# Recurrence steps of a two-layer hybrid block: products of even and odd heads placed in the two column halves of the array, with the state read directly

## The chip, the core and the metric

The kernel runs on one core of a Trainium2 chip. The metric is device time in microseconds (us) of one execution; lower is better. Three runs of the kernel before gave 2442.71, 2450.8 and 2458.3 us, a median of 2450.8 us.

## The reference

Two transformer layers run over 512 latent tokens and 256 context tokens of width 1024. Each layer has a mixing part (a WKV-7 recurrence with 8 heads of 64 in two directions, beside differential attention with 8 heads), an output projection, and a squared-ReLU MLP. All arithmetic is float32. The part that matters here is the recurrence, for each head and each direction:

```python
def step(state, inp):
    r_t, w_t, k_t, v_t, kk_t, b_t = inp
    sa = jnp.einsum("bhvk,bhk->bhv", state, kk_t)
    state = (state * w_t[:, :, None, :]
             - sa[..., :, None] * b_t[:, :, None, :]
             + v_t[..., :, None] * k_t[:, :, None, :])
    y = jnp.einsum("bhvk,bhk->bhv", state, r_t)
    return state, y
```

The context is scanned first and its last state starts the scan of the latent tokens. The second direction scans in reverse, and the two results are added. In the last layer the context's outputs are not needed.

## The kernel before, in words

**Chunks.** The recurrence does not go token by token. The 768 tokens are six blocks of 128 (`n` = 0 to 5), each two chunks of 64 (`j` = 0, 1). One call `step(n, j)` advances both directions (`d` = 0, 1) by one chunk, so a layer has 12 steps and 24 step-directions, and the program has 48. With the decays folded into the operands, a chunk is a few 64-wide matrix products and one triangular inverse per head.

**What is prepared.** `prep_a` and `prep_b` make a set of four tiles for each (n, d): `KR` (columns 0 to 63 hold the scaled kk, 64 to 127 the scaled r), `BN`, the decay column `dcv`, and `G`. `G` has, for each chunk and head, rows 64 to 127 for products with v, rows 0 to 63 for products with the solved u, columns 0 to 63 for the solve and 64 to 127 for y. There are six sets in turn, so block n + 3 writes where block n was. The upper left quarter of `G` must become the inverse of a unit triangular matrix: `relay` sends its diagonal blocks to DRAM, `inv` loads them with one system per partition, `eliminate` solves them by 30 pairs of vector operations (on POOL for n < 2, on DVE after), the result goes back through DRAM into rows 0 to 63 of `G` (L1137), and `merge` fills the off-diagonal block with 64 small matmuls and two copies (L1152 to L1165).

**One step.** For each direction:

- L1176 loads v into partitions 64 to 127 of `uv`, on SP's queue.
- L1186 multiplies rows 64 to 127 of `G` (64 rows of the array) by v for 8 heads, all into partitions 0 to 63 of the PSUM tile `X` (128 x 512), one head after the other along the free axis. The first of the 8 has 128 output columns, since it also clears the lower half.
- L1189 adds the state's part for two heads at a time: `KR` with 128 output columns (kk and r together) against `sbd`, a block diagonal copy of the state with 128 columns per pair of heads.
- L1192 copies the upper half of `X`, negated, into `xs` (one ACT operation of 64 x 512).
- L1198 applies the inverse to `xs`; even heads go to partitions 0 to 63 of a PSUM tile `us`, odd heads to 64 to 127. Two ACT copies (L1201) put the result into partitions 0 to 63 of `uv`.
- L1210 makes the state's increment, again with even and odd heads in the two halves; L1213 and L1215 (DVE) form the new state `sc`, and two ACT copies (L1218) refresh `sbd`.
- L1226 adds the products with u and v for y into partitions 64 to 127 of `X`; L1236 (ACT) or L1239 (DVE) takes y out.

**Order.** Each engine runs its instructions in a fixed order that a list scheduler made from the program's order and its own estimate of times. In the program, the steps are generators; at each of their pauses the code lets four pieces of `preps` go (for block n + 2) and, at the first pause of a step, four pieces of the modulation weights (`ada`, 0.5 MB each, matmuls at L265, loads at L254 on SP's queue, kept behind the load of v). `inv(n + 1)` stands ahead of block n's steps. `finish` normalizes y for a finished block and starts with the last additions to y; its transposes are L1288.

Of the kernel before, what the change touches and what calls it, by code (L numbers as in the profile page):

```python
# [164 lines left out]
class K:  # L165
# [760 lines left out]
    def recurrence(self, l, last, es, side):  # L926
# [7 lines left out]
        one = self.pool(es, "one", 1)  # L934
# [232 lines left out]
        def step(n, j):  # L1167
            need_y = not (last and n < 2)
            final = n == 5 and j == 1
            mw = 128 if need_y else 64  # L1170
            S = []
            for d in range(2):
                q = j if d == 0 else 1 - j
                t0 = tau(n, d) * 128 + q * 64
                uv = uvp.tile([128, 8, 64], F32, name=self.n("uv"), tag=f"uv{d}", bufs=2)
                ld = nc.sync.dma_start(uv[64:128], self.vnd[t0:t0 + 64, :].rearrange("t (h c) -> t h c", h=8))  # L1176
                self.gate = ld
                KR, BN, G, dcv = sets[(n, d)]
                S.append(dict(q=q, t0=t0, uv=uv, KR=KR, BN=BN, G=G, dc=dcv))
            for d in range(2):  # L1180
                s = S[d]
                q = s["q"]
                X = s["X"] = px[d].tile([128, 512], F32, name=self.n("X"), tag=f"X{d}")
                for h in range(8):
                    w = mw if h == 0 else 64
                    nc.tensor.matmul(X[0:w, h * 64:h * 64 + 64], s["G"][64:128, h - h % 2 + q, h % 2, 0:w],  # L1186
                                     s["uv"][64:128, h, :], start=(h == 0), stop=False, skip_group_check=True)
                for p in range(4):
                    nc.tensor.matmul(X[0:mw, p * 128:p * 128 + 128], s["KR"][:, 2 * p + q, 0:mw], sbd[:, d, p, :],  # L1189
                                     start=False, stop=False, skip_group_check=True)  # L1190
                xs = s["xs"] = xsd[d]
                nc.scalar.mul(xs[0:64], X[0:64, :], -1.0)  # L1192
                yield
            for d in range(2):
                s = S[d]
                up = us[:, d]
                for h in range(8):
                    nc.tensor.matmul(up[(h % 2) * 64:(h % 2) * 64 + 64, h // 2, :], s["G"][:, h - h % 2 + s["q"], h % 2, 0:64],  # L1198
                                     s["xs"][:, h * 64:h * 64 + 64], start=True, stop=True, skip_group_check=True)
                for hf in range(2):  # L1200
                    nc.scalar.copy(s["uv"][0:64, hf:8:2, :], up[hf * 64:hf * 64 + 64])  # L1201
                yield
            if not final:
                for d in range(2):
                    s = S[d]
                    q = s["q"]
                    sp = us[:, d]
                    for h in range(8):
                        hs = slice((h % 2) * 64, (h % 2) * 64 + 64)
                        nc.tensor.matmul(sp[hs, h // 2, :], s["BN"][:, h - h % 2 + q, hs], s["uv"][:, h, :],  # L1210
                                         start=True, stop=True, skip_group_check=True)
                    tt = uvp.tile([128, 4, 64], F32, name=self.n("st"), tag="st")
                    nc.vector.tensor_tensor(tt, sp, sc[d], ALU.add)  # L1213
                    dcv = s["dc"][:, q:8:2].unsqueeze(2).to_broadcast([128, 4, 64])
                    nc.vector.tensor_tensor(sc[d], tt, dcv, ALU.mult)  # L1215
                    for hf in range(2):
                        hs = slice(hf * 64, hf * 64 + 64)
                        nc.scalar.copy(sbd[hs, d, :, hs], sc[d][hs])  # L1218
                    yield
            if need_y:  # L1220
                for d in range(2):
                    s = S[d]
                    X = s["X"]
                    for h in range(8):
                        ks = slice(0, 64 if h == 0 else 128)
# [7 lines left out]
                    yo = Yt[hp * 64:hp * 64 + 64, :]  # L1233
                    if hp not in seen:
                        seen[hp] = 1
                        nc.scalar.copy(yo, X[64:128, :])  # L1236
                    else:
                        seen[hp] = 2
                        nc.vector.tensor_tensor(yo, X[64:128, :], yo, ALU.add)  # L1239
                    if len(seen) == 2 and min(seen.values()) == 2:  # L1240
                        done.append(ti)
                    yield

        def finish(ti):
# [57 lines left out]
            yield from inv(1)  # L1302

        def rest():
            nonlocal uvp, fp, px, us, xsd
# [3 lines left out]
            xsd = [uvp.tile([128, 512], F32, name=self.n("xs"), bufs=1) for _ in range(2)]  # L1309
# [5 lines left out]
            us = self.pool(es, "pus", 1, PSUM).tile([128, 2, 4, 64], F32, name=self.n("us"))  # L1315
            pms.append(self.pool(es, "pmr", 1, PSUM))
            ada = Fill()
            kinds = (("mix", "rows"), ("mlp", "cols"), ("mlp", "rows"))
            for kd, how in kinds:
                ada.add((self.ada_rows if how == "rows" else self.ada_cols)(l, kd, pa, "a"))  # L1320
            if l == 0:
                ada.add(self.ada_cols(1, "mix", pa, "a"))
            work = Fill()
            prep_until(1)
            for n in range(6):
                if n == 0:
                    merge(0)
                    merge(1)
                elif n < 5:
                    self.now(inv(n + 1))  # L1330
                for j in range(2):
                    nst = 0
                    for _ in step(n, j):
                        work(1)
                        if nst == 0:
                            with tc.issue_after(self.gate.ins):
                                ada(ADA[l])
                        nst += 1

# [12 lines left out]

        done, spare = [], []
        uvp = fp = px = us = xsd = None
        side.add(prologue())
        return rest

# [379 lines left out]
```

## Time and profile before

| | before |
|---|---|
| median of three runs | 2450.8 us |
| the profiled execution | 2465.64 us, span 2463.9 us |
| TensorE matmul busy, whole span | 92% |
| VectorE / ScalarE / GpSimd busy | 62% / 48% / 33% |
| 16 DMA engines | 127 GB/s mean |

The profile tells of one execution. Times in rows are from the start of its span. The steps of the first layer's recurrence run from about 490 to 763 us and those of the second layer's from about 1760 to 2047 us; windows with these bounds are used below. A float32 matmul appears as two records, so a group of 8 heads is "x16". Matmuls are pipelined: the start of one record to the start of the next tells how long it holds the array, while its shown duration includes its way through the array. PEclk is the granted TensorE clock as a share of 2.4 GHz; it takes one of two levels, 1.2 or 2.4 GHz, so a mean of 0.77 is a mixture of both.

### The profile page before, as it was taken

How to read it: one execution, taken by the hardware profiler on the slowest of the kernel's cores; microseconds unless marked ns; L12 is line 12 of the kernel's file. 1: busy time of each engine (PE TensorE's matmuls, PEld its weight loads, DVE VectorE, ACT ScalarE, POOL GpSimd, SP SyncE). 2: the span in 40 equal slices, each digit the busy share in tenths (PEclk: the TensorE clock that was granted, in tenths of full speed). 3: DMA queues.
4: the chain of work that ended last, by engine and by line, in shares of the span. 5: the costliest groups of instructions: out<-in, count | busy, mean ns of one | idle time of the engine just before them, and what ended most of it. 6: DMA issues, size and time to landing. Idle time of an engine off the chain costs nothing.

```text
span 2463.9 us, 43744 instructions
## 1 busy us (share of the span) xinstructions
PE 2273.2 (92%) x17150; PEld 1919.2 (78%) x17150; DVE 1516.6 (62%) x2629; ACT 1173.8 (48%) x2393; POOL 806.8 (33%) x1048
## 2 busy tenths in 40 slices
PE   6999998799989999999999989999989978999997
PEld 5887887677768988888888877788767758888886
DVE  5456458558654665555555646657556564778784
ACT  4345547554534543344343535547444444555452
POOL 1212324832111333333330422423641131553530
PEclk8999998798899999999999999999678879999998
DMA  7543535386687422221112354434566663423230
GB/s 270 154 129 94 133 110 140 74 228 172 148 208 236 152 77 69 69 69 61 60 61 85 124 164 122 122 108 115 148 158 158 166 161 137 161 91 117 87 119 35
DMA packets 291630, 313.67 MB, mean 127 GB/s; under 512 B 139680, under 2 KB 220896, under 8 KB 291424
## 3 DMA queue, kind: packets, MB, share of 16 engines
q1 hardware_dynamic: 280320, 284.66, 38.6%
q0 software_dynamic: 10240, 23.08, 5.0%
q8 instruction: 135, 2.21, 0.4%
q10 hardware_dynamic: 864, 3.15, 0.3%
q14 instruction: 71, 0.58, 0.1%
HBM read 257.04 MB, written 53.77 MB: 126 GB/s over the span
## 4 chain that ended last, share of the span: by engine, by line
PE 68%; DMA 10%; DVE 9%; ACT 4%; issue 3%; SPq 2%; POOL 2%; POOLq 0%; DVEq 0%; ACTq 0%
PE pf L351 31%; PE pu L351 15%; PE po L351 4%; DMA raw<-in_ada_w 2%; PE pb L1046 2%; PE po L832 2%; DMA TT<-dt 2%; PE X L1186 1%; PE pb L977 1%; PE adar L265 1%; PE sc L795 1%; DVE wl L1497 1%; PE X L1226 1%; DVE nm L797 1%; PE X L1189 1%
## 5 line engine op out<-in xcount | busy, mean ns | idle before, releaser
L1497 DVE TENSOR_TENSOR wl<-raw,wh 128x1024 fp32r<-128x1024 f32 x170 | 255.8, 1507 | 125.6 <-ACT wh L1496 124.8
L351 PE MATMUL pf<-hl,wh 128*128 128x512 f32 (+1 forms) x832 | 282.1, 342 | 0.0
L351 PE MATMUL pf<-hh,wh 128*128 128x512 f32 (+1 forms) x832 | 280.5, 342 | 0.5 <-ACT hh L397 0.5
L351 PE MATMUL pf<-hh,wl 128*128 128x512 f32 (+1 forms) x832 | 275.7, 342 | 0.0
L1496 ACT ACTIVATE wh<-raw 128x1024 fp32r<-128x1024 f32 x170 | 179.2, 1058 | 162.0 <-PE pf L351 143.9
L351 PE MATMUL pf<-wh,fah 128*128 128x512 f32 x570 | 225.3, 398 | 11.5 <-DVE fu L1630 7.2
L351 PE MATMUL pu<-hh,wh 128*128 128x512 f32 (+1 forms) x632 | 223.5, 354 | 4.8 <-DVE t L557 1.7
L351 PE MATMUL pf<-wl,fah 128*128 128x512 f32 x570 | 225.0, 396 | 0.7 <-DVE wl L1497 0.7
L351 PE MATMUL pf<-wh,fal 128*128 128x512 f32 x570 | 222.8, 397 | 1.8 <-DVE fal L1597 1.8
L351 PE MATMUL pu<-hh,wl 128*128 128x512 f32 (+1 forms) x632 | 218.1, 346 | 4.4 <-DVE wl L340 4.4
L351 PE MATMUL pu<-hl,wh 128*128 128x512 f32 (+1 forms) x632 | 217.8, 345 | 0.0
L797 DVE TENSOR_REDUCE nm<-sc 128x1 f32<-128x768 f32 (+1 forms) x160 | 132.6, 842 | 79.2 <-PE sc L795 78.5
L351 PEld LDWEIGHTS pf<-hl,wh 128*128 128x128 f32 x832 | 156.6, 188 | 20.0 <-DVE hl L399 0.2
L351 PEld LDWEIGHTS pf<-hh,wl 128*128 128x128 f32 x832 | 156.0, 188 | 20.0
L351 PEld LDWEIGHTS pf<-hh,wh 128*128 128x128 f32 x832 | 155.3, 188 | 20.4 <-ACT hh L397 0.8
L799 ACT ACTIVATE e<-sc,nm 128x768 f32<-128x768 f32 (+1 forms) x160 | 130.7, 821 | 53.7 <-DVE nm L797 44.3
L321 POOL TENSOR_TENSOR rs<-ms,pw 128x1 f32<-128x1 f32 (+2 forms) x60 | 56.8, 948 | 286.3 <-DVE ms L319 284.5
L351 PEld LDWEIGHTS pu<-hh,wh 128*128 128x128 f32 x632 | 121.0, 191 | 23.8 <-DVE t L557 2.3
L351 PEld LDWEIGHTS pf<-wh,fah 128*128 128x128 f32 x570 | 107.7, 189 | 38.9 <-ACT fah L1596 13.7
L1630 DVE TENSOR_TENSOR acc<-pf,acc 128x512 f32<-128x512 f32 x155 | 104.2, 682 | 53.9 <-PE pf L351 53.3
L351 PEld LDWEIGHTS pu<-hh,wl 128*128 128x128 f32 x632 | 120.7, 191 | 19.5 <-DVE wl L340 5.3
L351 PEld LDWEIGHTS pu<-hl,wh 128*128 128x128 f32 x632 | 120.8, 191 | 14.2 <-issue 1.7
(262 smaller groups left out, 5644.1 us busy)
## 6 DMA issues: line engine op xcount, KB each, us to landing
raw<-in_w_ff SPq DMA_DIRECT2D x128, 512.0 KB, 3.7
raw<-in_ada_w SPq DMA_DIRECT2D x96, 512.0 KB, 5.8
raw<-in_w_in SPq DMA_DIRECT2D x52, 512.0 KB, 4.6
ld<-zd SPq DMA_DIRECT2D x40, 384.0 KB, 3.9
ks<-qd POOLq DMA_DIRECT2D x64, 192.0 KB, 5.8
zd<-zr SPq DMA_DIRECT2D x22, 384.0 KB
raw<-in_w_out SPq DMA_DIRECT2D x16, 512.0 KB, 5.9
qs<-qd POOLq DMA_DIRECT2D x32, 192.0 KB, 6.0
```

Of the source, the lines that this page charges most:

```text
L265: nc.tensor.matmul(acc[32 * g:32 * g + 32, :], self.sc[:, 2 * kp + k, :], raw[:, k, g * 128:g * 128 + 128], start=(kp + k == 0), stop=(kp ...
L321: nc.gpsimd.tensor_tensor(r, m, self.pw1.to_broadcast([128, cols]), ALU.pow)
L351: nc.tensor.matmul(out, a, b, start=(start and i == 0 and j == 0), stop=(i == n - 1 and j == 2), skip_group_check=not start)
L795: nc.tensor.matmul(sc[:, k0:k1], qs[:, br, tk], ks[:, br, k0:k1], start=True, stop=True)
L797: nc.vector.tensor_reduce(nm, sc, AX.X, ALU.max, negate=True)
L799: nc.scalar.activation(ee, sc, AF.Exp, bias=nm, accum_out=ls[:, br:br + 1])
L832: nc.tensor.matmul(po, pT[:, k * 128:k * 128 + 128], vn[:, k, h * 64:h * 64 + 64], start=(k == 0), stop=(k == nk - 1))
L977: nc.tensor.matmul(pw[:, p, :, :], wab[:, d, cs], lt, start=True, stop=True, skip_group_check=True)
L1046: nc.tensor.matmul(pgt[:, u, 0:nn], BK[hs, u, :], KR[hs, 2 * pp + u, 0:nn], start=True, stop=True, skip_group_check=True)
L1496: nc.scalar.activation(hi, src, AF.Copy)
L1497: nc.vector.tensor_tensor(lo, src, hi.bitcast(F32), sub)
L1630: nc.vector.tensor_tensor(d, p, d, add)
```

## The change

The products of L1186 and of y are placed like those of L1198: even heads into partitions 0 to 63 and odd heads into 64 to 127, with all 128 rows of `G`; the u half of `uv` is first set to zero by POOL. The state's part is now eight products of 64 x 64 straight from `sc` (`from_state`), once for the solve and once for y; `sbd` and its copies go. The state has two buffers. Each direction has a PSUM bank that holds X and then u and the increment; y has a bank of its own, one for both directions. Y's layout in SBUF follows, and the transposes in `finish` become 16 products of 64 x 64.

```diff
-        sbd = one.tile([128, 2, 4, 128], F32, name=self.n("sbd"))
-        nc.gpsimd.memset(sbd, 0.0)
-        sc = [one.tile([128, 4, 64], F32, name=self.n("sc")) for _ in range(2)]
+        state = lambda d: one.tile([128, 4, 64], F32, name=self.n("sc"), tag=f"sc{d}", bufs=2)
+        sc = [state(d) for d in range(2)]
...
+                nc.gpsimd.memset(uv[0:64], 0.0)
...
+            def from_state(out, s, c0):
+                for h in range(8):
+                    hs = half(h)
+                    nc.tensor.matmul(out[hs, h // 2, :], s["KR"][hs, h - h % 2 + s["q"], c0:c0 + 64], s["old"][hs, h // 2, :],
+                                     start=False, stop=False, skip_group_check=True)
...
-                X = s["X"] = px[d].tile([128, 512], F32, name=self.n("X"), tag=f"X{d}")
+                X = s["X"] = px[d].tile([128, 2, 4, 64], F32, name=self.n("X"), tag=f"X{d}")
                 for h in range(8):
-                    w = mw if h == 0 else 64
-                    nc.tensor.matmul(X[0:w, h * 64:h * 64 + 64], s["G"][64:128, h - h % 2 + q, h % 2, 0:w],
-                                     s["uv"][64:128, h, :], start=(h == 0), stop=False, skip_group_check=True)
-                for p in range(4):
-                    nc.tensor.matmul(X[0:mw, p * 128:p * 128 + 128], s["KR"][:, 2 * p + q, 0:mw], sbd[:, d, p, :],
-                                     start=False, stop=False, skip_group_check=True)
+                    nc.tensor.matmul(X[half(h), 0, h // 2, :], s["G"][:, h - h % 2 + s["q"], h % 2, 0:64],
+                                     s["uv"][:, h, :], start=(h < 2), stop=False, skip_group_check=True)
+                from_state(X[:, 0], s, 0)
                 xs = s["xs"] = xsd[d]
-                nc.scalar.mul(xs[0:64], X[0:64, :], -1.0)
+                for hf in range(2):
+                    nc.scalar.mul(xs[0:64, hf], X[hf * 64:hf * 64 + 64, 0], -1.0)
...
-                up = us[:, d]
+                up = s["X"][:, 1]
...
+                    sc[d] = state(d)
                     nc.vector.tensor_tensor(sc[d], tt, dcv, ALU.mult)
-                    for hf in range(2):
-                        hs = slice(hf * 64, hf * 64 + 64)
-                        nc.scalar.copy(sbd[hs, d, :, hs], sc[d][hs])
...
-                    X = s["X"]
+                    Y = yp.tile([128, 4, 64], F32, name=self.n("Yb"), tag="Yb")
                     for h in range(8):
-                        ks = slice(0, 64 if h == 0 else 128)
-                        nc.tensor.matmul(X[64:128, h * 64:h * 64 + 64],
-                                         s["G"][ks, h - h % 2 + s["q"], h % 2, 64:128],
-                                         s["uv"][ks, h, :], start=False, stop=(h == 7), skip_group_check=True)
+                        nc.tensor.matmul(Y[half(h), h // 2, :], s["G"][:, h - h % 2 + s["q"], h % 2, 64:128],
+                                         s["uv"][:, h, :], start=(h < 2), stop=False, skip_group_check=True)
+                    from_state(Y, s, 64)
...
-                        nc.scalar.copy(yo, X[64:128, :])
+                        nc.scalar.copy(yo, Y)
...
-                nc.tensor.transpose(pt[:, p, :], Yt[:, p * 128:p * 128 + 128], self.ident)
+                for hp in range(2):
+                    for hf in range(2):
+                        hs = slice(hf * 64, hf * 64 + 64)
+                        c0 = hp * 256 + p * 64
+                        nc.tensor.matmul(pt[hs, p, hp * 64:hp * 64 + 64], Yt[hs, c0:c0 + 64], self.ident[hs, hs],
+                                         start=True, stop=True, skip_group_check=True)
```

## Rows read from the trace of the kernel before

**Rows 1.** Busy us (count) of PE, PEld, DVE, ACT, POOL; PEclk, DMA share, GB/s.

```profile
490.00:763.00 273.00, 244.22 (x3496) 195.72 (x3495) 170.63 (x463) 130.65 (x310) 69.59 (x122) 0.90 0.77 198
1760.00:2047.00 287.00, 248.31 (x3250) 203.85 (x3249) 158.96 (x435) 121.76 (x286) 80.39 (x170) 0.77 0.60 151
```

**Rows 2.** Chain of waits by line, 490 to 763, then 1760 to 2047.

```profile
by line: DMA raw<-in_ada_w 10.0%; PE pb L1046 7.3%; DMA TT<-dt 7.2%; PE X L1226 6.1%; PE adar L265 5.7%; PE X L1186 4.0%; PE pb L977 3.5%; DMA raw<-in_w_out 3.4%; DMA S<-gd 3.2%; DMA da<-S 3.0%; issue 3.0%; PE X L1189 2.9%; PE us L1198 2.9%
...
by line: PE X L1186 9.0%; PE adar L265 6.0%; PE pb L1046 5.8%; PE X L1189 5.7%; issue 5.1%; PE pb L977 5.0%; DMA TT<-dt 4.9%; DMA raw<-in_ada_w 4.6%; PE X L1226 4.3%; DMA S<-zd 4.1%; PE us L1198 3.7%; PE us L1210 2.9%; DVE pr L1100 2.9%; DM
```

**Rows 3.** Both stretches summed, for L1186, L1189, L1226 in this order.

```profile
sum 560.00, PE 77.20 PEld 64.68; mean PE 38.60 PEld 32.34
...
sum 560.00, PE 63.08 PEld 53.06; mean PE 31.54 PEld 26.53
...
sum 560.00, PE 56.06 PEld 47.00; mean PE 28.03 PEld 23.50
```

**Rows 4.** Timeline of PE, full clock: start, us, line, tiles, rows*columns, records.

```profile
704.97 0.69 PE L1210 MATMUL us<-uv,S 128*64 128x64 f32 x16
705.58 0.42 PE L265 MATMUL adar<-raw,sc 128*32 128x128 f32 x6
705.93 1.39 PE L1186 MATMUL X<-uv,S 64*128 64x64 f32 x16
707.25 2.05 PE L1189 MATMUL X<-sbd,S 128*128 128x128 f32 x16
...
713.98 0.32 PE L1226 MATMUL X<-uv,S 64*64 64x64 f32 x2
714.24 0.69 PE L1210 MATMUL us<-uv,S 128*64 128x64 f32 x16
714.76 0.98 PE L1226 MATMUL X<-uv,S 128*64 128x64 f32 x14
715.67 1.39 PE L1186 MATMUL X<-uv,S 64*128 64x64 f32 x16
```

**Rows 5.** Timeline of PE inside a merge, record by record.

```profile
691.33 0.19 PE L1154 MATMUL pg<-TT,S 32*32 32x32 f32 x1
691.34 0.19 PE L1152 MATMUL pg<-TT,S 32*32 32x32 f32 x1
691.36 0.19 PE L1154 MATMUL pg<-TT,S 32*32 32x32 f32 x1
```

**Rows 6.** Groups of ACT, 490 to 763: busy us, mean ns, idle before, releaser.

```profile
L1218 ACT COPY sbd<-sc 64x256 f32<-64x256 f32 x44 | 17.7, 402 | 19.9 <-DVE sc L1215 19.5
L1201 ACT COPY uv<-us 64x256 f32<-64x256 f32 x48 | 17.6, 366 | 18.2 <-PE us L1198 17.6
L1192 ACT ACTIVATE xs<-X 64x512 f32<-64x512 f32 x24 | 14.1, 586 | 20.9 <-PE X L1189 20.8
```

**Rows 7.** Line L1311, the memsets of 64x512: ns minimum, median, maximum.

```profile
L1311 POOL MEMSET xs<- x4: 519/519/519, 493.4 to 1756.1; 64x512 f32 x4
```

**Rows 8.** Waits: us in total, times, longest; first stretch, the last row second stretch.

```profile
PE X L1189 <- ACT sbd L1218: 3.1, 2, 2.2
...
SPq L1176 <- PE us L1210: 42.0, 15, 9.4
```

**Rows 9.** Timelines of ACT and PE around the first and the last late merge.

```profile
590.68 0.59 ACT L1192 ACTIVATE xs<-X 64x512 f32<-64x512 f32 x1 [2.38 <-PE X L1189]
...
604.71 0.58 ACT L1165 COPY S<-pg 32x512 f32<-32x512 f32 x1
...
607.39 0.69 PE L1198 MATMUL us<-xs,S 128*64 128x64 f32 x16
...
2004.60 0.59 ACT L1192 ACTIVATE xs<-X 64x512 f32<-64x512 f32 x1 [1.61 <-PE X L1189]
...
2024.90 0.58 ACT L1165 COPY S<-pg 32x512 f32<-32x512 f32 x1
...
2025.40 1.12 PE L1198 MATMUL us<-xs,S 128*64 128x64 f32 x16
```

More of the change, by code (lines that the diff above doesn't have):

```diff
@@ L1169, in step @@
             final = n == 5 and j == 1
-            mw = 128 if need_y else 64
             S = []
@@ L1177, in step @@
                 self.gate = ld
+                nc.gpsimd.memset(uv[0:64], 0.0)
                 KR, BN, G, dcv = sets[(n, d)]
-                S.append(dict(q=q, t0=t0, uv=uv, KR=KR, BN=BN, G=G, dc=dcv))
+                S.append(dict(q=q, t0=t0, uv=uv, KR=KR, BN=BN, G=G, dc=dcv, old=sc[d]))
+            half = lambda h: slice((h % 2) * 64, (h % 2) * 64 + 64)
+            def from_state(out, s, c0):
[3 more added lines that the diff above has]
+                                     start=False, stop=False, skip_group_check=True)
             for d in range(2):
                 s = S[d]
-                q = s["q"]
-                X = s["X"] = px[d].tile([128, 512], F32, name=self.n("X"), tag=f"X{d}")
+                X = s["X"] = px[d].tile([128, 2, 4, 64], F32, name=self.n("X"), tag=f"X{d}")
                 for h in range(8):
-                    w = mw if h == 0 else 64
-                    nc.tensor.matmul(X[0:w, h * 64:h * 64 + 64], s["G"][64:128, h - h % 2 + q, h % 2, 0:w],
-                                     s["uv"][64:128, h, :], start=(h == 0), stop=False, skip_group_check=True)
-                for p in range(4):
-                    nc.tensor.matmul(X[0:mw, p * 128:p * 128 + 128], s["KR"][:, 2 * p + q, 0:mw], sbd[:, d, p, :],
-                                     start=False, stop=False, skip_group_check=True)
+                    nc.tensor.matmul(X[half(h), 0, h // 2, :], s["G"][:, h - h % 2 + s["q"], h % 2, 0:64],
+                                     s["uv"][:, h, :], start=(h < 2), stop=False, skip_group_check=True)
+                from_state(X[:, 0], s, 0)
                 xs = s["xs"] = xsd[d]
-                nc.scalar.mul(xs[0:64], X[0:64, :], -1.0)
+                for hf in range(2):
+                    nc.scalar.mul(xs[0:64, hf], X[hf * 64:hf * 64 + 64, 0], -1.0)
                 yield
@@ L1195, in step @@
                 s = S[d]
-                up = us[:, d]
+                up = s["X"][:, 1]
                 for h in range(8):
-                    nc.tensor.matmul(up[(h % 2) * 64:(h % 2) * 64 + 64, h // 2, :], s["G"][:, h - h % 2 + s["q"], h % 2, 0:64],
-                                     s["xs"][:, h * 64:h * 64 + 64], start=True, stop=True, skip_group_check=True)
+                    nc.tensor.matmul(up[half(h), h // 2, :], s["G"][:, h - h % 2 + s["q"], h % 2, 0:64],
+                                     s["xs"][:, h % 2, h // 2, :], start=True, stop=True, skip_group_check=True)
                 for hf in range(2):
@@ L1206, in step @@
                     q = s["q"]
-                    sp = us[:, d]
+                    sp = s["X"][:, 1]
                     for h in range(8):
-                        hs = slice((h % 2) * 64, (h % 2) * 64 + 64)
-                        nc.tensor.matmul(sp[hs, h // 2, :], s["BN"][:, h - h % 2 + q, hs], s["uv"][:, h, :],
+                        nc.tensor.matmul(sp[half(h), h // 2, :], s["BN"][:, h - h % 2 + q, half(h)], s["uv"][:, h, :],
                                          start=True, stop=True, skip_group_check=True)
                     tt = uvp.tile([128, 4, 64], F32, name=self.n("st"), tag="st")
-                    nc.vector.tensor_tensor(tt, sp, sc[d], ALU.add)
+                    nc.vector.tensor_tensor(tt, sp, s["old"], ALU.add)
                     dcv = s["dc"][:, q:8:2].unsqueeze(2).to_broadcast([128, 4, 64])
+                    sc[d] = state(d)
                     nc.vector.tensor_tensor(sc[d], tt, dcv, ALU.mult)
-                    for hf in range(2):
-                        hs = slice(hf * 64, hf * 64 + 64)
-                        nc.scalar.copy(sbd[hs, d, :, hs], sc[d][hs])
                     yield
@@ L1232, in step @@
                     Yt, seen = ytiles[ti]
-                    yo = Yt[hp * 64:hp * 64 + 64, :]
+                    yo = Yt[:, hp * 256:hp * 256 + 256].rearrange("p (j c) -> p j c", j=4)
                     if hp not in seen:
                         seen[hp] = 1
-                        nc.scalar.copy(yo, X[64:128, :])
+                        nc.scalar.copy(yo, Y)
                     else:
                         seen[hp] = 2
-                        nc.vector.tensor_tensor(yo, X[64:128, :], yo, ALU.add)
+                        nc.vector.tensor_tensor(yo, Y, yo, ALU.add)
                     if len(seen) == 2 and min(seen.values()) == 2:
@@ L1304, in rest @@
         def rest():
-            nonlocal uvp, fp, px, us, xsd
+            nonlocal uvp, fp, px, yp, xsd
             side.drain()
@@ L1308, in rest @@
             uvp = self.pool(es, "uvp", 2)
-            xsd = [uvp.tile([128, 512], F32, name=self.n("xs"), bufs=1) for _ in range(2)]
+            xsd = [uvp.tile([128, 2, 4, 64], F32, name=self.n("xs"), bufs=1) for _ in range(2)]
             for x in xsd:
@@ L1314, in rest @@
             late["pg"] = lambda shape: pg.tile(shape, F32, name=self.n("pg"), tag="g")
-            us = self.pool(es, "pus", 1, PSUM).tile([128, 2, 4, 64], F32, name=self.n("us"))
+            yp = self.pool(es, "pyb", 1, PSUM)
             pms.append(self.pool(es, "pmr", 1, PSUM))
@@ L1353, in recurrence @@
         done, spare = [], []
-        uvp = fp = px = us = xsd = None
+        uvp = fp = px = yp = xsd = None
         side.add(prologue())
```

## The prediction

> **What bounds the kernel now.** The change touches the recurrence alone, so I first took the busy time of the two stretches that hold its steps [rows 1]. TensorE shows 244.2 of 273 us and 248.3 of 287 us, more than any other engine (DVE 170.6 and 159.0); the 16 DMA engines stand at 0.77 and 0.60, and the granted clock is 0.90 and 0.77. This looks like a stage bound by the array, but busy time is no proof, so the chain of waits comes next [rows 2]. In the first stretch the three matmul lines that the change rewrites carry 4.0 + 2.9 + 6.1 = 13.0% of 273 us, that is 35.5 us, beside DMA (modulation weights 10.0%, the inverse's `TT<-dt` 7.2%). In the second they carry 9.0 + 5.7 + 4.3 = 19.0% of 287 us, 54.5 us. So 90 us of the end depend on these lines, while they fill 77.2 + 63.1 + 56.1 = 196 us of the array [rows 3]: of a microsecond of their work saved, a little under half is worth time by the chain. The rest of the stage is latency: the inverse's way through DRAM, and weights that come late.
>
> **The array's work.** At full clock the starts of groups give the price of each [rows 4]. Eight products with even and odd heads in the two halves take 705.58 - 704.97 = 0.61 us (L1210). L1186, into one half, takes 707.25 - 705.93 = 1.32. L1189 takes 2.05 for both directions, 1.02 each. L1226 takes (714.24 - 713.98) + (715.67 - 714.76) = 1.17. A step-direction so pays 1.32 + 1.02 + 1.17 = 3.51 us. After the change it pays two groups over 128 rows (0.61 each, the row's own kind) and two `from_state` groups on 64 x 64 pieces on the diagonal of the array, which the trace does not show. Their bounds are 0.61, if the two pieces run beside each other, and 1.32, the price of L1186, if they take turns. Nearest are the merge's records: two pieces on the diagonal of 32 x 32 start 0.01 and 0.02 us apart though each shows 0.19 us [rows 5]. I take 0.61. Then 4 x 0.61 = 2.44 us replace 3.51, a share of 0.695, and of the 196 us some 60 go. On the chain that is 0.305 x 90 = **-27 us**; the bounds are -60, if the array is the whole bound, and 0, if other waits take it over.
>
> A rule speaks against this value. The merge's two pieces read different rows of the array and write one PSUM tile of 64 x 512, and they overlap [rows 5]. The Trainium skill, "TensorEngine Tiling (Array Packing)", section "Restrictions and Gotchas", says that different row tiles cannot use the same PSUM bank at the same time. Here even and odd heads are different row tiles of one bank, so by the rule `from_state` would take turns, and the sum would be that of the third rival below; the trace speaks against the rule for 32-row pieces, and no row shows 64-row ones.
>
> **The copies of the state.** 88 copies of 0.402 us [rows 6] leave ACT, 35 us. They stand between the new state and the next L1189, but PE had to wait for them only 3.1 us in the first stretch [rows 8]; I take about the same for the second: **-6 us**, with bounds of 0 and -35. Instead `xs` needs two operations of 64 x 256 (0.366 each, L1201's price) for one of 0.586: 0.15 us more, 48 times, 7 us, of which under half on the chain: **+3**. Y's exit works on 128 x 256 instead of 64 x 512 and gets shorter; other work covers it, 0.
>
> **The wait that is added.** X used to read rows 64 to 127 of `G` only, so L1186, L1189 and `xs` of a block's first chunk ran while the inverse was still on its way. Now X reads rows 0 to 63 as well (times the zeros of `uv`), and these are what `merge` and its loads write: X must wait for the merge. The ACT and PE timelines show where it was used as cover. In the first layer's block 2 the first `xs` of the pair that waits starts at 590.68, the merge's last copy is at 604.71 and L1198 starts at 607.39; in the second layer's block 5 the second `xs` is done at 2005.19, the copy is at 2024.90, L1198 at 2025.40 [rows 9]. I count seven such blocks of twelve, these being the first and the last: 2 to 5 in the first layer, 0, 1 and 5 in the second. In each, X and the state's part (2 x 0.61), the way out of the array (about 0.3: 0.69 shown for a group that holds it 0.61, and the wake of ACT) and two ACT operations (0.73) now follow the merge: 2.3 us. PE's order has other work at some of these places, the queue behind L1198 being prep and modulation products. 7 x 2.3 = 16; I take **+12**. Bounds: 0, and 12 x 3.5 = 42 with every block late and the array at half clock.
>
> **The rest.** POOL gets 48 memsets of 0.519 us [rows 7], 25 us, under its idle 203 and 207 us [rows 1]. They wait for `uv` to come free, as the load of v does, which held up SP's queue for 42.0 us in the second stretch, up to 9.4 at once [rows 8]; behind a memset on POOL stand prep's operations, and behind those the next relay. In the second layer's start POOL also solves the block 1 system, and four memsets there delay it by 2 us. I take **+2**, bounds 0 and 15. Y's bank is shared by the directions: the second y waits for the exit of the first, about 0.6 us; L1210 and L1186 of the other direction stand between the groups today [rows 4]: **+2**, bounds 0 and 16 (20 pairs by 0.8). `KR` is now read until y, so prep of block n + 3 may write later: **+2**, bounds 0 and 10. The transposes in `finish` are 32 records in pairs instead of 8 full ones, 0. SP issues the same loads; v comes at the same place in its queue.
>
> **Sum.** -27 - 6 + 3 + 12 + 2 + 2 + 2 = -12 us. The profiled execution took 2465.6 us (span 2463.9), 15 us above the median of the runs, so its 2465.6 - 12 = 2453.6 stands for 2450.8 - 12 = **2439 us** in a median run. About 1%, 24.5 us, is what counts as a difference here.
>
> **Rivals.**
>
> - **The array was the whole bound.** For it: 89% and 87% busy, and the order of PE is so full that any shorter group lets the next start. Against: the chain gives these lines less than half. The 60 us come whole: -60 - 6 + 3 + 12 + 6 = -45, 2406 us. Chance 0.25.
> - **The merge becomes the gate of every block (slower).** Place: first X of each block. For it: the inverse's DMA steps are on the chain with 7.2% and 4.9%, and seven blocks wait already. Since X no longer runs ahead, the idle array also loses clock and the saved work is only what was idle anyway: 42 - 6 + 3 + 6 - a tenth of 60 saved = about +39, 2490 us. It decides when the merge ends after the previous block's last state in most blocks; in five of the twelve it ended earlier before the change. Chance 0.15.
> - **The diagonal pieces take turns.** Then a step-direction costs 2 x 0.61 + 2 x 1.32 = 3.86 against 3.51; +0.35 by 48 is +17 us of array time, +8 on the chain: 8 - 6 + 3 + 12 + 6 = +23, 2474 us. Against it are the merge's records. Chance 0.08.
> - **Weights and the inverse's loads set the pace.** The array gets shorter and waits longer for `in_ada_w` and `TT<-dt`: -27 becomes about -8, and the added wait is hidden too: about 2446 us. DMA at 0.77 speaks for it. Chance 0.14.
>
> My own sum has 0.38, with a range of its own from 2420 to 2455.
>
> **How the numbers follow.** Faster by over 1% (under 2426): the first rival and a fifth of my own case, 0.33. Slower by over 1% (over 2475): most of the second rival and half of the third, 0.17. Within: 0.50. The range must take in the better half of the first rival's and the lower part of the second's outcomes: 2398 to 2482.
>
> **What would show it.** Right: 16-record groups of X and y that hold the array some 0.6 us, `from_state` too; no ACT copies behind L1215; X of a block's first chunk starting right behind the merge's copies; recurrence stretches together 5 to 25 us shorter, the rest unchanged. Wrong: `from_state` records 0.06 us apart one by one (third rival); a granted clock in the stretches clearly under 0.90 and 0.77, with PE idle ahead of X (second); stretches 40 us or more shorter with PE as busy as before (first); PE's waits for `in_ada_w` grown by what the products saved (fourth). A POOL queue in which a memset holds back prep would upset the sum most.

## The result, and the profile after

The changed kernel takes 2489.5 us (median of four runs, 2484.2 to 2492.5), the kernel before 2449.1 us (2442.7 to 2458.3). The ratio is 1.0169, with a 95% interval from 1.0137 to 1.0200: slower by 1.7%, where 2439 us and a range up to 2482 had been predicted.

The products themselves became what was forecast. This is the timeline of TensorE (PE) after, with the columns of [rows 4]:

```profile
523.10 0.68 PE L1186 MATMUL Yb<-sc,S 64*64 64x64 f32 x16
523.71 0.69 PE L1193 MATMUL X<-uv,S 128*64 128x64 f32 x16
524.32 0.68 PE L1186 MATMUL X<-sc,S 64*64 64x64 f32 x16
524.93 0.43 PE L265 MATMUL adar<-raw,sc 128*32 128x128 f32 x8
```

A group of products over 128 rows and a group on 64 x 64 diagonal pieces each hold the array for 0.61 us from start to start (523.10, 523.71, 524.32, 524.93). Lines L1186 (now `from_state`), L1193 (X with v) and L1228 (y) answer to [rows 3]; the windows are 490 to 785 and 1760 to 2076:

```profile
sum 611.00, PE 75.89 PEld 59.62; mean PE 37.94 PEld 29.81
...
sum 611.00, PE 42.19 PEld 33.68; mean PE 21.09 PEld 16.84
...
sum 611.00, PE 36.85 PEld 29.73; mean PE 18.43 PEld 14.87
```

That is 154.9 us in place of 196.3: 41 us less by busy time, where the prediction had 60. The stretches got longer all the same. Here are their busy times as in [rows 1]; first the kernel before over the longer windows that the changed kernel needs, then the changed kernel:

```profile
490.00:785.00 295.00, 266.22 (x3677) 217.54 (x3677) 181.32 (x483) 140.38 (x330) 75.54 (x126) 0.91 0.73 192
1760.00:2076.00 316.00, 267.65 (x3387) 222.74 (x3387) 172.54 (x455) 132.31 (x305) 86.26 (x174) 0.77 0.58 152
```

```profile
490.00:785.00 295.00, 234.55 (x4127) 188.30 (x4126) 172.77 (x480) 117.81 (x296) 78.75 (x140) 0.82 0.65 171
1760.00:2076.00 316.00, 233.86 (x3792) 193.16 (x3792) 182.07 (x472) 123.45 (x305) 116.20 (x249) 0.76 0.57 140
```

In the first 295 us PE is busy 32 us less, of which 18 us are the rewritten lines themselves, and DVE, whose work the change hardly touches, 9 us less: the first layer's stage is further back with everything. In the second window DVE shows 9.5 us more. The chain of waits of these two windows, beside [rows 2]:

```profile
by line: issue 8.9%; DMA raw<-in_ada_w 8.5%; DVE pr L1100 4.3%; PE adar L265 4.3%; DVE W L1102 4.2%; DMA TT<-dt 4.1%; DMA dn<-W 3.3%; PE pb L977 3.0%; DMA raw<-in_w_out 2.9%; DMA dt<-R 2.6%; DMA frk<-gd 2.5%; DMA S<-zd 2.3%; PE pb L1046 2.2
...
by line: DMA raw<-in_ada_w 11.8%; issue 8.6%; PE pb L1046 7.1%; PE X L1193 4.2%; PE X L1186 3.6%; PE adar L265 3.3%; PE Yb L1186 3.2%; PE X L1215 3.1%; PE pb L977 3.1%; PE po L351 2.7%; PE X L1204 2.7%; DMA N<-da 2.6%; PE Yb L1228 2.5%; DMA
```

In the first window the rewritten products are no longer among the largest shares; the elimination (L1100, L1102) and the inverse's transfers (`dn<-W`, `dt<-R`, `TT<-dt`) are. In the second they still carry 4.2 + 3.6 + 3.2 + 2.5 = 13.5%, where it was 19.0% before. The ACT groups beside [rows 6] (no copies of the state, two operations for `xs`) and PE's and POOL's longest waits in the first window (us in total, times, longest; beside [rows 7, 8]):

```profile
L1198 ACT ACTIVATE xs<-X 64x256 f32<-64x256 f32 x48 | 18.2, 378 | 20.9 <-PE X L1186 20.4
L1207 ACT COPY uv<-X 64x256 f32<-64x256 f32 x48 | 17.6, 366 | 6.6 <-PE X L1204 5.7 <-issue 0.2
```

```profile
PE adar L265 <- DMA raw<-in_ada_w: 15.5, 10, 3.9
PE pg L1152 <- DMA TT<-dt: 8.7, 5, 4.2
PE pb L1283 <- POOL S L1281: 6.1, 2, 5.4
PE adar L265 <- DVE W L1102: 5.1, 1, 5.1
PE X L1204 <- ACT xs L1198: 5.0, 1, 5.0
...
POOL uv L1177 <- PE Yb L1228: 65.5, 10, 23.5
```

No single wait of PE holds the 40 us. Where they arise is read from marks in each trace: the starts of the first and the last record of the output projection (`po`, L351), in us from the span's start, and the end of the second layer's first merge. The last two columns are differences of such marks.

| kernel | `po`, layer 1 | merge(0), layer 2 | last `po`, layer 2 | span | last `po` to merge(0) | merge(0) to last `po` |
|---|---|---|---|---|---|---|
| before | 761 to 843 | 1800 | 2102 | 2463.9 | 957 | 302 |
| after | 778 to 857 | 1827 | 2125 | 2485.8 | 970 | 298 |
| e4 | 753 to 832 | 1796 | 2085 | 2445.5 | 964 | 289 |
| e7 | 757 to 842 | 1794 | 2094 | 2455.5 | 952 | 300 |
| e17 | 794 to 874 | 1841 | 2133 | 2495.0 | 967 | 292 |
| e18 | 779 to 859 | 1819 | 2121 | 2481.7 | 960 | 302 |

After against before, 14 us are lost up to the end of the first layer's output projection, and 13 in the stretch that holds the first layer's MLP and the second layer's attention, beside which the recurrence is prepared. From the second layer's first merge on nothing more is lost (298 against 302). But the traced execution of the kernel before took 2465.6 us, 17 more than its median, so this pair of traces shows only 22 of the 40 us. The safer pair is e7 (below: the same products with the old banks), whose trace, like that of the changed kernel, is within 2 us of its median: against it 15 us are lost up to the output projection's end, 18 in the stretch behind it, and nothing after (298 against 300). The first layer's steps themselves end only 2 us later than in e7: the last product for y is done at 771.9 against 769.9 us. In the first layer the tail of the recurrence is plain to see (PE, then ACT, with the idle time ahead of an instruction and its releaser in brackets):

```profile
742.40 0.33 PE L1295 MATMUL pb<-cst,Y 64*64 64x64 f32 x2 [0.79 <-DVE Y L1278]
748.14 2.07 PE L1283 MATMUL pb<-S,cst 128*128 128x512 f32 x2 [5.42 <-POOL S L1281]
750.14 1.97 PE L1295 MATMUL pb<-cst,Y 64*64 64x64 f32 x30
752.04 1.12 PE L1204 MATMUL X<-xs,S 128*64 128x64 f32 x16
```

```profile
744.08 0.63 ACT L1274 ACTIVATE S<-Y 128x512 f32<-128x512 f32 x1 [5.44 <-issue]
744.73 0.78 ACT L1198 ACTIVATE xs<-X 64x256 f32<-64x256 f32 x2
```

The second direction's `xs` stands on ACT behind `finish`'s square, its solve (L1204) on PE behind `finish`'s product (L1283), which waits for POOL. That looked like the cause; e21 below speaks against it.

### The profile page after: what moved, and what is told of

The parts are those of the page before. It is cut to its first block, busy times and chain, and to the rows that moved or that the text cites. A ratio compares the mean times of both kernels' runs of the same rounds, so it can differ in the third digit from the quotient of the medians.

```text
span 2485.8 us, 46409 instructions
## 1 busy us (share of the span) xinstructions
PE 2232.2 (90%) x18454; PEld 1885.6 (76%) x18454; DVE 1514.2 (61%) x2629; ACT 1143.7 (46%) x2353; POOL 820.8 (33%) x1094
## 4 chain that ended last, share of the span: by engine, by line
PE 66%; DMA 10%; DVE 10%; issue 5%; ACT 4%; POOL 3%; SPq 1%; DVEq 0%; ACTq 0%; POOLq 0%
PE pf L351 31%; PE pu L351 15%; PE po L351 4%; DMA raw<-in_ada_w 3%; PE po L832 2%; PE pb L1046 2%; PE sc L795 1%; DVE wl L1505 1%; PE adar L265 1%; PE pb L977 1%; PE ptr L815 1%; POOL pr L1100 1%; POOL W L1102 1%; DVE nm L797 1%; DVE pr L1100 1%
## 5 line engine op out<-in xcount | busy, mean ns | idle before, releaser
L351 PE MATMUL pf<-hl,wh 128*128 128x512 f32 (+1 forms) x832 | 282.2, 342 | 0.0
L351 PE MATMUL pf<-hh,wh 128*128 128x512 f32 (+1 forms) x832 | 280.5, 342 | 0.6 <-ACT hh L397 0.6
L351 PE MATMUL pf<-hh,wl 128*128 128x512 f32 (+1 forms) x832 | 275.5, 342 | 0.0
L351 PE MATMUL pf<-wh,fah 128*128 128x512 f32 x570 | 225.2, 398 | 13.5 <-DVE fu L1638 7.2
L351 PE MATMUL pu<-hh,wh 128*128 128x512 f32 (+1 forms) x632 | 224.2, 355 | 4.6 <-DVE t L557 1.7
L351 PE MATMUL pf<-wl,fah 128*128 128x512 f32 x570 | 224.3, 395 | 0.5 <-DVE wl L1505 0.5
L351 PE MATMUL pf<-wh,fal 128*128 128x512 f32 x570 | 222.1, 395 | 1.8 <-DVE fal L1605 1.8
L351 PE MATMUL pu<-hh,wl 128*128 128x512 f32 (+1 forms) x632 | 218.3, 346 | 3.8 <-DVE wl L340 3.8
L351 PE MATMUL pu<-hl,wh 128*128 128x512 f32 (+1 forms) x632 | 218.3, 345 | 0.0
L351 PEld LDWEIGHTS pf<-hl,wh 128*128 128x128 f32 x832 | 156.6, 188 | 20.0 <-DVE hl L399 0.2
L351 PEld LDWEIGHTS pf<-hh,wl 128*128 128x128 f32 x832 | 156.0, 188 | 19.9
L351 PEld LDWEIGHTS pf<-hh,wh 128*128 128x128 f32 x832 | 155.3, 188 | 20.4 <-ACT hh L397 0.8
L351 PEld LDWEIGHTS pf<-wh,fah 128*128 128x128 f32 x570 | 107.6, 189 | 41.0 <-ACT fah L1604 13.7
L351 PEld LDWEIGHTS pu<-hh,wh 128*128 128x128 f32 x632 | 120.9, 191 | 23.0 <-DVE t L557 2.4
L351 PEld LDWEIGHTS pu<-hh,wl 128*128 128x128 f32 x632 | 120.9, 192 | 19.1 <-DVE wl L340 4.7
L351 PEld LDWEIGHTS pu<-hl,wh 128*128 128x128 f32 x632 | 121.1, 192 | 14.4 <-issue 1.7
```

The lines of the kernel that those rows point to most:

```text
L351: nc.tensor.matmul(out, a, b, start=(start and i == 0 and j == 0), stop=(i == n - 1 and j == 2), skip_group_check=not start)
```

## The experiments

All times are medians. The changed kernel is at 2489.5 us, the kernel before at 2449.1 us in the first comparison and 2451 to 2458 in the others; ratios are to the kernel before.

**e4, the wait and the memset alone, in the kernel before.** The forecast of a slower kernel rested on the wait for the merge.

```diff
+                nc.gpsimd.memset(uv[0:64], 0.0)
-  nc.tensor.matmul(X[0:w, ...], s["G"][64:128, h - h % 2 + q, h % 2, 0:w], s["uv"][64:128, h, :], ...)
+  nc.tensor.matmul(X[0:w, ...], s["G"][:, h - h % 2 + q, h % 2, 0:w], s["uv"][:, h, :], ...)
```

> The kernel before with one thing of the change: the products of L1186 read all 128 rows of G, times a uv whose upper half POOL has zeroed. So it has the wait for the merge and the memset, and none of the rest. Theories A and B together: 2475 to 2500 us. Theories C and D: 2445 to 2460, since neither Y's bank nor the array's work is touched.

2447.7 us, ratio 0.9982 (0.9950 to 1.0013). The wait and the memset, both in full, cost the kernel before nothing that can be measured, though POOL waits 37.3 us for `uv` in the first window. A and B fall as causes by themselves.

**e1, a tile for the inverse; e16, the same with the banks of e7.** `merge` and the loads at L1137 write to a tile `Gi` of their own and L1204 reads it; R and other small tiles share buffers to make room.

```diff
-  nc.sync.dma_start(Gs[d][bs, :, bs], dn[...])
+  nc.sync.dma_start(own(n, d)[0][bs, :, bs], dn[...])
-  nc.tensor.matmul(up[...], s["G"][:, ..., 0:64], s["xs"][:, h % 2, h // 2, :], ...)
+  nc.tensor.matmul(up[...], own(n, d)[0][:, ..., 0:64], s["xs"][ps, h % 2, h // 2, :], ...)
```

> The inverse gets a tile of its own (all blocks but block 1), so that X, which still reads rows 0 to 63 of G times zeros, no longer waits for the merge; the memset on POOL, Y's shared bank and all else of the change stay. Theory A (the added wait of X for the merge made the 40 us): the loss comes back and the shorter products show, 2415 to 2455 us. Theory B (the memset that waits in POOL's queue): 2480 to 2500, no change against the changed kernel. Theory C (Y's one bank for both directions): 2480 to 2500. Theory D (the saved array time only reshuffled the order at the stretch's end, late weights and finish): 2475 to 2495.

> e7 with a tile of its own for the inverse in all blocks but block 1, so that X doesn't wait for the merge. Theory L1 (the wait takes what the shorter products save): 2415 to 2440 us. Theory L2 (the saved array time is idle time anyway): 2450 to 2465. The tile's first filling and its buffer cost a few us at most.

2503.8 us (1.0181, 1.0151 to 1.0211) and 2524.2 us (1.0290, 1.0225 to 1.0355). e1 lies outside A's range, but neither tells A from the rest or L1 from L2: in both the edit also changes what the solve computes, in a way that stays unexplained, and takes buffers from other tiles, and both are slower than the kernels that they start from. So the price of the wait inside the changed kernel stays open.

**e3, the memset on DVE.**

```diff
-                nc.gpsimd.memset(uv[0:64], 0.0)
+                nc.vector.memset(uv[0:64], 0.0)
```

> The changed kernel with the memset of uv's upper half on DVE in place of POOL; X still waits for the merge. Theory A: 2480 to 2500, as the changed kernel. Theory B: POOL's queue is free again, 2440 to 2465, though DVE then carries the wait for uv. Theory C: 2480 to 2500.

2496.4 us (1.0160, 1.0121 to 1.0199). With the memset gone from POOL's queue, and with it the 65.5 us of waiting for `uv`, the loss stays. The queue is not the cause.

**e5, y in four banks in turn; e10, three buffers of uv; e11, y in X's bank; e12, y ahead of the increment.** These aim at y. In the changed kernel y follows its solve after 9.6 us on average in the first layer, before it was 3.8.

```diff
e5:  -  Y = yp.tile([128, 4, 64], ...)      +  Y = bank([128, 2, 4, 64])[:, 0]
e10: -  uv = uvp.tile(..., bufs=2)          +  uv = uvp.tile(..., bufs=3)
e11: -  Y = yp.tile([128, 4, 64], ...)      +  Y = s["X"][:, 0]
e12: "if need_y:" moved ahead of "if not final:"
```

> The changed kernel with y in four PSUM banks that it takes in turn with the preparation's products, in place of one bank for both directions. Theory C: 2445 to 2470. Theories A, B and D: 2480 to 2500.

> The changed kernel with three buffers of uv per direction in place of two. In the trace of the changed kernel y comes 9.6 and 6.9 us behind its solve (first, second layer) where it came 3.8 and 3.2 us behind it before, since nothing any longer needs it out of X's bank. Theory J1 (the late y costs the time because it holds uv, and so the memset in POOL's queue and the load of v in SP's): 2450 to 2470 us. Theory J2 (it holds KR and the set, which a third uv doesn't help): 2475 to 2500. Theory J3 (not the late y, but that u and the increment lie in X's bank): 2480 to 2500.

> The changed kernel with y in the half of its direction's bank that X leaves; u and the increment stay in the other half of the same bank, and no further bank is used. So y must be out before the next X of its direction, as before the change. Theories J1 and J2 (late y): 2450 to 2470 us, y 3 to 5 us behind its solve. Theory J3 (u and the increment in X's bank): 2480 to 2500.

> The changed kernel, banks as changed, but y is written in the program ahead of the increment, so that the scheduler sets it earlier; it puts up to 1.2 us of products ahead of each state. Theories J1 and J2: 2455 to 2480 us. Theory J3: 2485 to 2510.

2497.5 us (1.0157, 1.0122 to 1.0192), 2484.3 (1.0117, 1.0078 to 1.0156), 2492.7 (1.0147, 1.0107 to 1.0186) and 2491.6 (1.0144, 1.0108 to 1.0179). e11 does not test the late y as I meant it, since y follows after 9.6 us there too; in e12 it follows after 6.4 us, and nothing is gained. C falls, and e10 gives back some 5 us, which is all that shows of J1. What all these kernels share is that u and the increment lie in X's bank. They also share a late y: 6.4 us in e12, 7.9 or more in the others, against 3.8 before.

**e7, the banks as before.** u and the increment in one bank shared by both directions, y in the other half of its X's bank; all else is as changed.

```diff
-  up = s["X"][:, 1]                +  up = us[:, d]
-  sp = s["X"][:, 1]                +  sp = us[:, d]
-  Y = yp.tile([128, 4, 64], ...)   +  Y = s["X"][:, 1]
-  yp = self.pool(es, "pyb", 1, PSUM)
+  us = self.pool(es, "pus", 1, PSUM).tile([128, 2, 4, 64], F32, name=self.n("us"))
```

> The changed kernel with the PSUM banks as before: u and the increment in one bank shared by the directions, y in the bank of its direction's X. Theory H (the order of the accesses to the new banks makes the loss): 2440 to 2465 us. Theories E, F, G: 2480 to 2505.

2456.0 us (1.0025, 1.0003 to 1.0047): 33.5 of the 40 us are the banks, as theory H forecast. Its trace has the same low clock in the first stretch as the changed kernel, 0.82:

```profile
490.00:785.00 295.00, 258.45 (x4357) 210.76 (x4354) 177.02 (x484) 124.78 (x310) 85.67 (x147) 0.82 0.69 178
```

Over whole runs the clock differs a little. The changed kernel's four runs have a mean granted clock of 0.922 to 0.926, e7's ten 0.923 to 0.935, and the three of e7 in 0.923 to 0.927 took 2460 to 2465 us, against 2484 to 2492. So some 25 of the 33.5 us remain at the same clock.

**e17 and e18, one of the two in X's bank.** From e7, only the increment (e17) or only u (e18) goes back.

```diff
e17: -  sp = us[:, d]    +  sp = s["X"][:, 0]
e18: -  up = us[:, d]    +  up = s["X"][:, 0]
```

> The banks as before (e7), but the increment in the half of the bank of X that X leaves; u stays in the bank shared by the directions, y in the other half of X's bank. Theory K1 (the next X, and y, can't start until DVE has read the increment, which before could go on beside them): 2475 to 2500 us. Theory K2 (u in X's bank is what costs): 2450 to 2465.

> The banks as before (e7), but u in the half of the bank of X that X leaves; the increment stays in the bank shared by the directions. Theory K1: 2450 to 2465 us. Theory K2: 2475 to 2500. If both e17 and e18 stay at 2450 to 2465, it is the sum of the two, or that y has a bank of its own.

2496.2 us (1.0169, 1.0111 to 1.0226) and 2484.8 us (1.0124, 1.0063 to 1.0184). Either one alone brings back most of the loss, against both K1 and K2 as they were put. In both y is late as well (9.6 and 8.6 us behind its solve in the first layer, 4.4 in e7), so these runs don't part the held bank from the late y. What the banks permit is seen at the second layer's start, where no y is needed (PE: X's products with v, u, the increment, and at the end the state's part for the next step; e7 first, then the changed kernel):

```profile
1793.86 1.12 PE L1193 MATMUL X<-uv,S 128*64 128x64 f32 x16 [3.18 <-DVE S L1164]
1795.97 1.12 PE L1193 MATMUL X<-uv,S 128*64 128x64 f32 x16
1797.75 0.69 PE L1204 MATMUL us<-xs,S 128*64 128x64 f32 x16
1798.27 1.13 PE L1193 MATMUL X<-uv,S 128*64 128x64 f32 x32
1799.48 0.69 PE L1204 MATMUL us<-xs,S 128*64 128x64 f32 x16
1801.01 0.69 PE L1215 MATMUL us<-uv,S 128*64 128x64 f32 x16 [0.85 <-ACT uv L1207]
1810.39 1.12 PE L1215 MATMUL us<-uv,S 128*64 128x64 f32 x16 [8.69 <-DVE st L1218]
1811.44 0.80 PE L1186 MATMUL X<-sc,S 64*64 64x64 f32 x10
```

```profile
1826.32 1.12 PE L1193 MATMUL X<-uv,S 128*64 128x64 f32 x16 [3.89 <-DVE S L1164]
1828.42 1.12 PE L1193 MATMUL X<-uv,S 128*64 128x64 f32 x16
1830.52 2.00 PE L1204 MATMUL X<-xs,S 128*64 128x64 f32 x32
1832.49 0.69 PE L1215 MATMUL X<-uv,S 128*64 128x64 f32 x16
1833.37 0.69 PE L1215 MATMUL X<-uv,S 128*64 128x64 f32 x16 [0.20 <-ACT uv L1207]
1838.07 1.12 PE L1193 MATMUL X<-uv,S 128*64 128x64 f32 x16 [4.02 <-DVE st L1218]
1839.12 1.12 PE L1186 MATMUL X<-sc,S 64*64 64x64 f32 x16
```

In e7 the next step's X (1798.27) runs between the two solves, as soon as `xs` has been read. After the change it waits for L1218 to read the increment (1838.07): u and the increment hold the bank that X needs. Yet at this place the run-ahead gains nothing: in e7 the second direction's increment waits 8.69 us for L1218 (1810.39), and the state's part for the next step comes 17.6 us after the step's first X (1811.44 - 1793.86), in the changed kernel 12.8 (1839.12 - 1826.32). The mean time from a step's increment to the next X of the second layer is 3.4 us in e7 (in the kernel before X is 3.9 us ahead of it), 11.2 in the changed kernel and in e17, 7.9 in e18. So a run-ahead is lost. But the table says that this stretch of the second layer takes no longer for it, and in the first layer, where y holds the bank anyhow, the mean is the same (8.7 in e7, 8.6 after). In e4 the time from increment to X grows too, from 2.2 to 6.4 us in the first layer and from -3.9 to 1.9 in the second, at no cost. The lost run-ahead is shown; that it is the way in which the 33 us arise is not.

**e14, e7 with three buffers of uv.**

```diff
-  uv = uvp.tile(..., bufs=2)          +  uv = uvp.tile(..., bufs=3)
```

> The changed kernel with the banks as before (e7) and three buffers of uv. POOL's memset still waits for uv 25 us and SP's load of v too in e7. If these waits hold back the preparation and the loads behind them: 2425 to 2445 us, faster than both kernels. If other work covers them: 2450 to 2460, as e7.

2462.9 us (1.0041, 1.0020 to 1.0062): no gain, so the waits for `uv` are covered.

**e6 and e19, X's products with v three times.**

```diff
-  for h in range(8):         +  for h in [*range(8)] * 3:
```

> The changed kernel with X's products with v made three times over (each pass starts the sums anew), so that a step-direction takes 6 x 0.61 = 3.66 us of the array, as much as before the change (3.51); 48 x 1.22 = 59 us of array work are put back. Theory E (the stage is bound by the latency of the inverse and the preparation; the array time that the change saves turns into idle time, and idle time costs granted clock, so that all other products take longer): 2440 to 2475 us, faster than the changed kernel in spite of more work, with half-clock time in the first recurrence back from about 100 us towards 53. Rival F (latency alone, no help from the clock): 2490 to 2505. Rival G (the array is still the bound, the loss comes from elsewhere): 2510 to 2550.

> e7 with X's products with v made three times over, which puts 59 us of array work back, about as much as the change saved. Theory L1, the array is on the path: 2485 to 2505 us, as in e6. Theory L2 (idle time anyway): 2455 to 2470.

2535.2 us (1.0318, 1.0267 to 1.0368), 45.7 more than the changed kernel, and 2499.0 us (1.0186, 1.0116 to 1.0256), 43.0 more than e7, as L1 had it. Theory E, which had e6 faster than the changed kernel, falls, and F with it. Over the same window the busier array is granted no more in e6 (0.79 against 0.82), but a little more in e19 than in e7 (0.84 against 0.82; columns of [rows 1], e6 and then e19):

```profile
490.00:785.00 295.00, 243.75 (x4492) 204.08 (x4490) 156.63 (x447) 107.63 (x273) 69.93 (x134) 0.79 0.56 146
...
490.00:785.00 295.00, 250.57 (x4831) 209.49 (x4828) 159.96 (x460) 113.52 (x288) 80.20 (x144) 0.84 0.63 164
```

The added work costs about three quarters of its 59 us. It does not say that the saved work is worth as much, since these products stand between `uv` and the solve, and so lengthen the way of each step.

**e8 and e9, half of the elimination's rounds left out**, in the changed kernel and in the one before.

```diff
-            for t in range(1, 31):
+            for t in range(1, 31, 2):
```

> The changed kernel with every second of the 30 rounds of the elimination left out (so the inverse is not the inverse). Theory E or F (the inverse's latency sets the pace after the change): 2440 to 2470, 20 to 50 us off. Rival G: 2475 to 2495.

> The kernel before with the same 15 rounds left out. Theory E or F: the array is more of the bound here, so it gains clearly less than the changed kernel does, 2430 to 2450. If the inverse set the pace before the change as well, 2400 to 2430, as much off as in the changed kernel.

2428.8 us (0.9897, 0.9855 to 0.9939) and 2432.3 us (0.9918, 0.9878 to 0.9957). The changed kernel gains 60.7 us, the one before some 19, and they meet. With less of the elimination (which frees DVE as well) the loss is gone, and with it theory G, which e6 had seemed to bear out; e8 falls below the range of E and F too. In the first layer of e8 y is as late (10.2 us) and X as long behind the increment (8.5 us) as in the changed kernel, so neither makes it slower than e9 by itself. This fits a stage that with the new banks waits more for the inverse and for DVE, as the chain of the first window has it, but doesn't prove it.

**e20 and e21, the first layer's tail.** `finish` held behind the last block's steps; and six pieces of modulation weights per step in place of four.

```diff
e20: -  work(1)            +  if n < 5: work(1)
e21: -  ADA = [4, 4]       +  ADA = [6, 4]
```

> The changed kernel, with no piece of finish let go between the steps of the last block (in both layers); it all comes behind them. Theory M (the tail's order: xs waits on ACT, the second solve on PE and the last weights on SP behind instructions of finish that aren't ready): 2460 to 2480 us, with the last modulation product of the first layer at 755 to 765 in place of 774. Rival N (the tail is late because the last block's state is late): 2485 to 2505, the tail as long or longer.

> The changed kernel with six pieces of the modulation weights let go at each step of the first layer in place of four, so that the last ones are used before the last block's steps. Theory M: the output projection no longer waits for them and starts some 15 us earlier, 2465 to 2480 us. Rival N: it then waits for the last tokens or for the output weights, 2485 to 2500.

2504.8 us (1.0214, 1.0166 to 1.0263) and 2499.3 us (1.0202, 1.0143 to 1.0261). In e20 the scheduler still put products of `finish` ahead of the second solve, and PE waits as long as before (PE, as above):

```profile
749.29 2.08 PE L1283 MATMUL pb<-S,cst 128*128 128x512 f32 x2 [5.49 <-POOL S L1281]
751.30 0.69 PE L1295 MATMUL pb<-cst,Y 64*64 64x64 f32 x6
...
752.91 1.03 PE L1204 MATMUL X<-xs,S 128*64 128x64 f32 x16
```

In e21 the last weights were used early, the output projection started at 750, and it still ended at 864, later than the 857 of the changed kernel:

```profile
709.73 1.08 PE L265 MATMUL adar<-raw,sc 128*32 128x128 f32 x16 [5.54 <-DMA raw<-in_ada_w]
...
750.35 0.58 PE L351 MATMUL po<-wh,hh 128*128 128x256 f32 x1
...
863.66 0.29 PE L351 MATMUL po<-wh,hl 128*128 128x256 f32 x1
```

Theory M falls with e21; e20 did not change the order that it was meant to change.

No version with the change and the reference's whole computation is faster than the kernel before; e7 is the best form of the change, 0.25% behind it.

## Why the prediction was wrong

**The array's work: price right, worth not.** Four groups of 0.61 us replaced 3.51, as worked out, and the diagonal 64 x 64 pieces overlap. So the third rival is out. The rule that stood behind it (the Trainium skill, "TensorEngine Tiling (Array Packing)", "Restrictions and Gotchas": different row tiles can't use one PSUM bank at the same time) is not borne out by the trace for pieces in different rows and different columns: 0.61 us for the 16 records into one tile. By busy time the lines fell by 41 us, not 60; at the chain's share of 90 in 196 the -27 would have been -19. The stretches did not get shorter, so the first rival is out as well. What the saving is worth can be bounded only in e7, which has it without the new banks: e7 is 4.5 us slower than the kernel before, where my terms without Y's bank give -14. Some 19 us of that sum did not come. Most of them go with the clock, for which my sum has no term: over whole runs e7 is granted 0.931 (median of ten), the kernel before 0.938 (median of 54). At the same clock, 0.930 to 0.935, the kernel before took 2463 us (median of 12 runs) and e7 2454 (median of 6), 9 us less. That the saved array work is what lowers the clock is not shown: with work put back e19 was granted 0.931 to 0.938, but e6 no more than the changed kernel in the first window. No run takes apart the -27, the wait's +12 and the -6 + 3 of the copies.

**The wait that is added.** In the kernel before, wait and memset together came to -3.7 us, which is within the noise, against forecasts of 12 and 2 (e4): mis-sized there. The steps that I counted as running ahead of a late merge must have had slack behind them. Inside the changed kernel its price is open.

**The rest: the step that failed.** Of the banks I costed only that the directions share Y's, at +2 us. That "each direction has a PSUM bank that holds X and then u and the increment" I did not cost at all, and there 33.5 us lie (e7), with either of the two products enough for most of it (e17, e18). The rows that could have made me ask are [rows 9] with [rows 4]: products for X ran ahead while other products of the steps were under way, and the bank decides whether they can. I had credited the run-ahead to the rows of `G` that X reads alone.

**The second rival** had the time, 2490 us, but not the cause. Its place was the merge; e4 and e7 both keep that wait and are at 2448 and 2456. Its clock is in the trace (0.82 against 0.91 in the same window), but e7 has it too, without the loss. Its time was right by luck.

**The fourth rival**, at 2446 us, had for its sign that PE's waits for `in_ada_w` grow by what the products saved. They grew from 15.0 to 17.8 us and those for `TT<-dt` from 2.9 to 8.7 (480 to 870 us), far less than 41.

**POOL's queue**, named as what would upset the sum most, waited 65.5 us for `uv` in the first window and cost nothing that e3 could give back.

**Open** is by what way the banks cost 33 us. Each engine's order is fixed by a list scheduler; a different bank changes what may run when, and can so change the order of the whole stage. Shown are that run-ahead is lost and y comes late, the places where the time goes, and that a shorter elimination makes the loss vanish. No run joins these into one chain, since no run held the order still while the banks changed.

## What to carry to other kernels

When a result moves to another buffer, ask for every tile what its next user now waits for, and price that like an instruction: a bank that frees early lets the next step's work run ahead, and a layout that saves array time can take that away. Whether that costs time is another question, which only a run answers. Try such a change in parts on the chip, with products and buffers apart; here the products were harmless and the banks were not. Where an added wait looks dear because work ran ahead of it, put that wait alone into the old kernel first: here it cost nothing. And before two traces are compared, see how far each execution is from its kernel's median: here the trace of the kernel before was 17 us slow.

## What was not expected of the hardware

`from_state` on two diagonal 64 x 64 pieces, which accumulate into one PSUM tile, costs no more than products over all 128 rows (0.61 us for 16 records each). And the granted clock goes with the time within one kernel, but does not rank kernels: the 54 runs of the kernel before that stand beside the experiments go from 2437 us at a mean clock of 0.948 to 2459 to 2471 us at 0.930 to 0.932, while the stretch from 490 to 785 us shows 0.82 both in the changed kernel at 2489.5 us and in e7 at 2456.0.
